# Another order of the first FFN weight loads, and another home for two addends, in a fused decoder layer

## The chip, the cores and the metric

The kernel runs on one core of a Trainium2 chip. A core has a matmul engine (TensorE, PE in the profile, with its weight loads PEld), three engines for other arithmetic (VectorE or DVE, ScalarE or ACT, GpSimd or POOL) and a queue engine (SyncE or SP) that issues DMAs. DMAs are issued from the queues of SP, POOL and, here and there, ACT; each engine and each queue takes its own instructions in order, and semaphores connect them.

The metric is the device time of one execution in microseconds, the median over several runs.

## The reference

One layer of a decoder: 512 tokens of 1024 channels, in float32. An attention branch and a pooling branch are gated, projected and added to the input, then normed. What the change touches lies in the second half, the gated MLP:

```python
a, u = jnp.split(h @ w_ffn_in[l], 2, axis=-1)          # 1024 -> 2 x 2816
a = causal_dwconv(a, conv_w[l], conv_b[l])             # width 3 along the tokens
f = (jax.nn.gelu(a, approximate=False) * u) @ w_ffn_out[l]
h = layer_norm(ALPHA * h + f, ln2_g[l], ln2_b[l])
```

## The kernel before

**Precision.** A float32 operand is cut into a rounded part `hi` (by ScalarE) and the rest `lo` (by VectorE, which needs `hi`). A product is three matmuls: hi·hi, hi·lo, lo·hi (`mm3`, line 287). Each weight tile is thus split on its way: ScalarE's `whi<-...` and then VectorE's `wlo<-...` in the profile, into one of five slots (`RING`).

**FFN, first matmul.** The 2816 channels are 22 tiles of 128. For tile f there are a weight tile `a` and a weight tile `u`; f = 0 is computed in the plain way (line 1162), and f = 1 to 21, the pairs, by a scheme with seven block products in place of eight (`seven`, line 336, and, with every step written out by hand, `Begun`, line 1333, for the pairs 1 to 3). With 1 and 2 for the halves of the 1024 input channels, the weights of a pair are

- A = [a1, a2], loaded as it is (line 213),
- X = [u1 + a1, u1 + u2], made by two DMAs: SP loads u1 twice (line 223), and then POOL issues an accumulating DMA that adds a1 and u2 from memory (line 225). The second waits until the first has landed,
- D = u2, loaded by SP (line 217),
- Y = [a1 + u1 + u2, a1 + a2 + u1 + u2], formed by VectorE in A's tile from X's second half (`form_y`, line 231; `half_sum` in the hand-written part).

A block product of 128 input channels and 256 tokens is 12 matmuls of 256 columns. The products of a pair are two with A, two with X, two with Y and one with D; they run into two PSUM banks, and between two products into the same bank ScalarE or VectorE takes out what stands there (lines 341 to 356, and 1339 to 1363). What ScalarE takes out of A's first product is an addend `y`, which VectorE adds to the bank later (lines 356 and 1360).

**Order.** From line 1122 to line 1405 VectorE, ScalarE and TensorE keep the order in which the program names their instructions (`VEC.on = ACT.on = TEN.on`); after it, and on the DMA queues throughout, a planner orders the instructions by times that it estimates. `tc.issue_after` and data dependences bind it. `more()` (line 1141) splits the next weight tile.

**Where the weights of the pairs lie.** The output of the first matmul is `fT`, 22 rows of 128x512. Pairs 1 to 4 use rows of it that are written late: `tail` (line 1213) gives them rows 19, 16, 13 and 10, two for X and the next one for D. The space of `fT` is free when the last matmul of the projection before it has run. From pair 5 on X lies in one of two tiles `xraw` and D in `draw`, in space that is free after line 1320. The loads of pairs 1 and 2 are issued by line 1227; those of pairs 3 and 4 come up as the weights before them are split (line 180). Line 1304 writes one element of pair 3's X tile by a memset in VectorE's order, so that the DMA, which overwrites it, waits for VectorE to come that far.

**Where the addends lie.** Pairs 1 to 4 keep `y` in `fT` (`first`, line 1229), pairs 5 to 21 in the two halves of a tile `p1` (128x512).

**FFN, second matmul.** Line 1417 onward: again seven products, of 11 x 6 matmuls of 512 columns each (`product`, line 1465). The first, B11, has its weights loaded into six pieces `tw` (line 1331, `load_walk`): two tiles of their own, the two `xraw`, `tw4`, which takes the space of `nT1`, and last `p1`, the sixth and half as large (in the profile `p`). From each piece, once it is split, an accumulating DMA makes the weights of the next such product. The second product's weights come through three buffers `wraw` (line 273). Another set of tiles, `t3`, is loaded during the third product (line 1451); its last piece is `t3_end`, 128x512, made at line 1327 and not used until then.

Of the kernel before, what the change touches and what calls it, by code (L numbers as in the profile page):

```python
# [17 lines left out]
D = 1024  # L18
# [5 lines left out]
NF = DFF // P  # L24
# [25 lines left out]
COVER = 2  # L50
# [23 lines left out]
def layer_kernel(ctx: ExitStack, tc: tile.TileContext, xT, x, w_v, w_c, rel_bias, invcnt, w_group,  # L74
                 pscale, w_br, w_out, lnr, w_fi, convp, w_fo, out):
    nc = tc.nc
    VEC, ACT, TEN = (InLine(tc, e) for e in (nc.vector, nc.scalar, nc.tensor))
# [27 lines left out]
    first = {"q": 0, "k": 4, "p": 8, "g": 12}  # L105
# [96 lines left out]
    coming = {q: list(pair_of) for q in "DAX"}  # L202
# [6 lines left out]
    def fetch_raw(key, q):  # L209
        a, u = pair_of[key]  # L210
        r = raws[key, q] = homes[key[0], q](key[1])
        if q == "A":
            ins = nc.sync.dma_start(r, a)
            if key == ("f", COVER // 2 + 3):
                state["A5"] = ins
        elif q == "D":
            state["D", key] = nc.sync.dma_start(r, u[:, S:])
        elif key in SUMMED:
            state["plain"] = nc.sync.dma_start(r[:, :S], u[:, :S])
        else:  # L220
            v = r.rearrange("p (a c) -> p a c", a=2)
            (pst, pn), (est, _) = u.ap
            state["plain"] = nc.sync.dma_start(
                v, bass.AP(tensor=u.tensor, offset=u.offset, ap=[[pst, pn], [0, 2], [est, S]]))
            state["acc"] = nc.gpsimd.dma_start(  # L225
                v, bass.AP(tensor=a.tensor, offset=a.offset, ap=[[pst, pn], [u.offset + S - a.offset, 2], [est, S]]),
                accum_op=ALU.add)
# [108 lines left out]
    def seven(key, whole, tt, y, u, done, between=None, begun=None, turned=False):  # L336
        ba, bc = begun or seven_a(key, whole, y)
        bb = bank(f"sb{key[0]}{key[1]}")
        chain, low, c11 = ba[:, 256:], bb[:, :256], bc[:, :256]

        def b_(k, t):
            return whole[0][:, k, t], whole[1][:, k, t]

        flush()
        s_mm(key, "X", 0, tt["T3"], low, True)
        state["low"] = nc.scalar.activation(u[:, t2], low, AF.Copy, scale=-1.0 if turned else 1.0)
        s_mm(key, "Y", 0, tt["nT2"], chain, False)
        state["Y0"] = state["mm"]
        nc.scalar.activation(u[:, t1], chain, AF.Copy)
        s_mm(key, "D", 0, tt["T4"], low, False)  # L350
        nc.vector.tensor_tensor(u[:, t1], u[:, t1], low, op=ALU.add)
        if between:
            between()
        s_mm(key, "X", 1, tt["nT1"], chain, False, between or key == ("f", NF - 1))
        nc.vector.tensor_tensor(u[:, t2], u[:, t2], chain, op=ALU.subtract if turned else ALU.add)
        state["add"] = added[key] = nc.vector.tensor_tensor(ba[:, t1], y, c11, op=ALU.add)

        def close():
            s_mm(key, "Y", 1, b_(k2, t2), chain, False, between or key == ("f", NF - 1))
            done(ba, u)  # L360

        pending.append(close)
# [558 lines left out]
    def gate_done(f, ba, u):  # L921
        if f < KT - 1:
            for br, v, scale in ((0, ba, 1.0), (1, u, -1.0)):
                nc.scalar.activation(v, v, AF.Sigmoid, scale=scale)
                nc.vector.tensor_tensor(branch[f, br], branch[f, br], v, op=ALU.mult)
            merged(f, branch[f, 0], branch[f, 1])
            unused.append(branch[f, 1])
        else:
            for br, v, scale in ((0, ba, 1.0), (1, u, -1.0)):
                gslot[8 * br + f] = unused.pop(0)  # L930
                nc.scalar.activation(gslot[8 * br + f], v, AF.Sigmoid, scale=scale)
# [6 lines left out]
    for f in range(GSEVEN, KT):  # L938
        if f == KT - 1:
# [3 lines left out]
              lambda ba, u, f=f: gate_done(f, ba, u), first_half if f == KT - 1 else None)  # L943
# [218 lines left out]
    def fi_mm(j, b, t, pin=False):  # L1162
        wh, wl = split3(weights(at["f", j // 2, "au"[j % 2]]), KT)
        for kt in range(KT):
            mm3(b[:, t], (wh[:, kt, :], wl[:, kt, :]), (hT_hi[:, kt, t], hT_lo[:, kt, t]), kt == 0, kt == KT - 1,
                pin and kt == 0)
# [18 lines left out]
    def gated(j, a, u, sign=None):  # L1185
        gate_begin(j, a)
        gate_end(j, u, sign)
# [25 lines left out]
    tail = {COVER // 2 + n: NF - 3 * (n + 1) for n in range(4)}  # L1213

    def x_home(f):
        if f in tail:
            return fT[:, tail[f]:tail[f] + 2, :].rearrange("p a c -> p (a c)")
        return xraw[f % 2]
# [2 lines left out]
        return fT[:, tail[f] + 2, :] if f in tail else draw[:, f % 2 * S:(f % 2 + 1) * S]  # L1221

    homes["f", "X"], homes["f", "D"] = x_home, d_home
    for f in list(tail)[:2]:
        for q in "XD":
            coming[q].remove(("f", f))
            fetch_raw(("f", f), q)

    def first(f):
        n = min(tail.values()) - 1 - f // 2 % 2  # L1230
        return fT[:, n, f % 2 * 256:f % 2 * 256 + 256]
# [26 lines left out]
    def low(i, *names):  # L1258
        for n in names:
            lows[n, i]()  # L1260
# [40 lines left out]
        begin_seven(2)  # L1301
    half_sum(1, 0)
    fi_mm(0, hb[0], t2)
    VEC.memset(x_home(COVER // 2 + 2)[:, :1], 0.0)
    state["mid"] = [lambda: low(2, "T4")]
    more()
    high(3, "nT2")
# [16 lines left out]
    p1 = xu.tile([P, S], F32, name="p1")  # L1324
    tw = [xu.tile([P, D], F32, name=f"tw{n}") for n in range(2)]
    tw += [xraw[(NF - 2) % 2], xraw[(NF - 1) % 2], p1]
    t3 = [xu.tile([P, S], F32, name="t3_end")]

    def load_walk(*which):
        for c in which:  # L1330
            state["walk"] = nc.sync.dma_start(tw[c], half("B11", piece(c)))
# [74 lines left out]
    pending.append(before.close)  # L1406
    state["limit"] = len(chunks) - 1
    for f in SEVEN[BEGUN:]:
        y = first(f) if f in tail else p1[:, f % 2 * 256:f % 2 * 256 + 256]
        if f == NF - 2:  # L1410
            with tc.issue_after(state["D", ("f", f - 1)].ins):
                load_walk(0, 1)
        elif f == NF - 1:
            load_walk(2)
        seven(("f", f), (hT_hi, hT_lo), tt, y, fT[:, f, :], lambda ba, u, f=f: gated(f, ba, u, -1.0),
              turned=f < KH)
# [205 lines left out]
```

## Time and profile before

| | us |
|---|---|
| median of 3 runs | 619.1 |
| the three runs | 615.93, 619.1, 621.42 |
| the profiled execution | 623.8 |
| its span, first to last instruction | 622.1 |
| TensorE busy | 608.5 |
| VectorE busy | 526.5 |
| ScalarE busy | 371.8 |
| POOL busy | 132.8 |
| mean granted TensorE clock | 0.997 of full speed |

A profile's numbers belong to one execution, which is a little longer than the three runs shown. A row of a timeline gives the start (us from the start of the span), the duration, the engine, the line, the operation and what it writes and reads; in brackets stands how long the engine was idle before and what ended that. Line 67 is a helper that records the instructions of the hand-ordered engines, so for most rows the names of the tiles tell the place: `sa..`, `sb..` are the two banks of a pair, `fi` those of tile 0, `foa` to `foe` and `fol` those of the second matmul. In the hand-ordered part each copy into `fT` is an output or an addend of a pair. A row of the chain gives start, duration and what was on it; for a DMA, from its issue to its landing. A row of a window gives the stretch, its length, the busy time of PE, PEld, DVE, ACT and POOL with their numbers of instructions, the granted clock, the busy share of the DMA engines and GB/s.

Matmuls are pipelined in the profile: a row's duration is longer than the distance to the next row's start.

### The profile page before, as it was taken

The numbers are of one execution on the slowest core, as the hardware profiler recorded it, in microseconds if no ns is written. First come the engines' busy times: TensorE is split into PE (matmuls) and PEld (weight loads), VectorE is DVE, ScalarE is ACT, GpSimd is POOL, SyncE is SP. The second block draws the span as 40 slices with busy tenths as digits, with TensorE's granted clock in tenths as the row PEclk, the third lists the DMA queues.
The fourth block names the chain that finished last, engine by engine and source line by source line (L and its number), as shares of the span: only waits on it lengthen the run. The fifth ranks groups of instructions, "written<-read, shape, count | busy, mean of one in ns | idle before, by whom it ended". The sixth has DMA issues, their size and how long they took to land.

```text
span 622.1 us, 11141 instructions
## 1 busy us (share of the span) xinstructions
PE 608.5 (98%) x4317; PEld 550.8 (89%) x4317; DVE 526.5 (85%) x808; ACT 371.8 (60%) x573; POOL 132.8 (21%) x149
## 2 busy tenths in 40 slices
PE   9999999999999999999979999999999999999995
PEld 6899898777899998889979999999999996788885
DVE  6978886868879888789969989999998985999995
ACT  6536667567556655445645666666666664755761
POOL 0133207350512111101110111102122121542110
PEclk9999999999999999999999999999999999999998
DMA  8667654147877235906692677677897687999424
GB/s 318 217 189 195 170 161 144 36 156 233 215 188 175 53 130 179 365 3 207 144 224 87 167 190 193 189 208 177 210 262 199 174 179 170 330 211 210 95 38 98
DMA packets 44228, 110.24 MB, mean 177 GB/s; under 512 B 4480, under 2 KB 6408, under 8 KB 44176
## 3 DMA queue, kind: packets, MB, share of 16 engines
q0 software_dynamic: 16576, 39.74, 32.9%
q1 hardware_dynamic: 27168, 69.15, 32.5%
q8 instruction: 34, 0.56, 0.4%
q10 hardware_dynamic: 432, 0.66, 0.3%
q14 instruction: 18, 0.15, 0.1%
HBM read 105.96 MB, written 3.69 MB: 176 GB/s over the span
## 4 chain that ended last, share of the span: by engine, by line
PE 89%; DMA 6%; DVE 2%; issue 1%; ACT 1%; SPq 0%; ACTq 0%; POOLq 0%
PE saf L67 21%; PE sbf L67 8%; PE br L67 7%; PE wo L67 7%; PE sag L67 6%; PE fod L67 5%; DMA fT<-in_w_fi 5%; PE foa L67 5%; PE sai L67 5%; PE sbg L67 3%; PE foe L67 3%; PE v L480 3%; PE sbi L67 2%; PE g L67 2%; PE p L67 2%; PE scg L67 2%
## 5 line engine op out<-in xcount | busy, mean ns | idle before, releaser
L67 ACT ACTIVATE whi<-araw 128x1024 fp32r<-128x1024 f32 x62 | 65.4, 1059 | 28.5 <-PE saf L67 14.1
L67 DVE TENSOR_TENSOR wlo<-araw,whi 128x1024 fp32r<-128x1024 f32 x62 | 75.8, 1242 | 6.2 <-ACT whi L67 4.3
L67 PE MATMUL saf<-hT_hi,whi 128*128 128x256 f32 x252 | 70.5, 280 | 0.7 <-DVE fT L67 0.7
L67 PE MATMUL saf<-hT_lo,whi 128*128 128x256 f32 x252 | 70.0, 278 | 0.0
L67 PE MATMUL saf<-hT_hi,wlo 128*128 128x256 f32 x252 | 69.8, 277 | 0.0
L225 POOL DMA_DIRECT2D xraw<-in_w_fi x17 | 20.4, 1197 | 145.7 <-DMA xraw<-in_w_fi 72.3
L67 PE MATMUL saf<-nT_hi,whi 128*128 128x256 f32 x168 | 46.7, 278 | 2.2 <-ACT fT L67 2.2
L67 DVE TENSOR_TENSOR wlo<-wraw,whi 128x1024 fp32r<-128x1024 f32 (+1 forms) x33 | 38.8, 1184 | 11.3 <-ACT whi L67 11.1
L67 PEld LDWEIGHTS saf<-hT_hi,whi 128*128 128x128 f32 x252 | 47.3, 188 | 1.0 <-DVE fT L67 0.9
L67 PEld LDWEIGHTS saf<-hT_lo,whi 128*128 128x128 f32 x252 | 47.3, 188 | 0.0
L67 PEld LDWEIGHTS saf<-hT_hi,wlo 128*128 128x128 f32 x252 | 47.3, 188 | 0.0
L67 PE MATMUL saf<-nT_lo,whi 128*128 128x256 f32 x168 | 46.8, 279 | 0.0
L67 PE MATMUL saf<-nT_hi,wlo 128*128 128x256 f32 x168 | 46.7, 278 | 0.0
L67 ACT ACTIVATE whi<-wraw 128x1024 fp32r<-128x1024 f32 (+1 forms) x33 | 33.0, 1015 | 17.9 <-DMA wraw<-in_w_out 7.5
L67 PE MATMUL sbf<-T_lo,whi 128*128 128x256 f32 x144 | 40.1, 278 | 0.0
L67 PE MATMUL sbf<-T_hi,whi 128*128 128x256 f32 x144 | 40.0, 278 | 0.0
L67 PE MATMUL sbf<-T_hi,wlo 128*128 128x256 f32 x144 | 39.9, 277 | 0.0
L67 ACT ACTIVATE whi<-xraw 128x1024 fp32r<-128x1024 f32 x25 | 26.4, 1061 | 18.6 <-PE saf L67 13.9
L67 PEld LDWEIGHTS saf<-nT_hi,whi 128*128 128x128 f32 x168 | 31.5, 188 | 2.4 <-ACT fT L67 2.4
L67 DVE TENSOR_TENSOR wlo<-xraw,whi 128x1024 fp32r<-128x1024 f32 x25 | 30.7, 1233 | 1.3 <-ACT whi L67 0.2
L67 PEld LDWEIGHTS saf<-nT_hi,wlo 128*128 128x128 f32 x168 | 31.5, 188 | 0.0
L67 PEld LDWEIGHTS saf<-nT_lo,whi 128*128 128x128 f32 x168 | 31.5, 188 | 0.0
(455 smaller groups left out, 2111.1 us busy)
## 6 DMA issues: line engine op xcount, KB each, us to landing
araw<-in_w_fi SPq DMA_DIRECT2D x19, 512.0 KB, 4.1
xraw<-in_w_fi SPq DMA_DIRECT2D x17, 512.0 KB, 5.9
xraw<-in_w_fi POOLq DMA_DIRECT2D x17, 512.0 KB, 7.1
araw<-in_w_c SPq DMA_DIRECT2D x12, 512.0 KB, 5.2
tw<-in_w_fo POOLq DMA_DIRECT2D x9, 512.0 KB, 9.3
draw<-in_w_fi SPq DMA_DIRECT2D x17, 256.0 KB, 3.6
wraw<-in_w_br SPq DMA_DIRECT2D x8, 512.0 KB, 4.2
wraw<-in_w_out SPq DMA_DIRECT2D x8, 512.0 KB, 4.0
```

Source lines behind the costliest of these rows:

```text
L67: ins = call(*a, **kw)
L225: state["acc"] = nc.gpsimd.dma_start(v, bass.AP(tensor=a.tensor, offset=a.offset, ap=[[pst, pn], [u.offset + S - a.offset, 2], [est, S]]), ...
L480: ins = nc.tensor.matmul(bs[j], xs_[j][a], (wh, wl)[b], start=kt == 0 and n == 0, stop=False)
```

## The change

Three edits.

1. The loop that issues the loads of pairs 1 and 2 (X1 with its accumulation, D1, X2, D2) now issues those of pairs 1 to 3 in the order X1, X2, D1, X3, D2, D3.
2. The memset of line 1304 writes into pair 4's X tile instead of pair 3's, so that pair 4's load waits for it.
3. The addends of the pairs 20 and 21 lie in `t3[0]`, which at that place is `t3_end`, instead of `p1`.

```diff
     homes["f", "X"], homes["f", "D"] = x_home, d_home
-    for f in list(tail)[:2]:
-        for q in "XD":
-            coming[q].remove(("f", f))
-            fetch_raw(("f", f), q)
+    for q, n in (("X", 0), ("X", 1), ("D", 0), ("X", 2), ("D", 1), ("D", 2)):
+        key = ("f", COVER // 2 + n)
+        coming[q].remove(key)
+        fetch_raw(key, q)
...
-    VEC.memset(x_home(COVER // 2 + 2)[:, :1], 0.0)
+    VEC.memset(x_home(COVER // 2 + 3)[:, :1], 0.0)
...
     for f in SEVEN[BEGUN:]:
-        y = first(f) if f in tail else p1[:, f % 2 * 256:f % 2 * 256 + 256]
+        home = p1 if f < NF - 2 else t3[0]
+        y = first(f) if f in tail else home[:, f % 2 * 256:f % 2 * 256 + 256]
```

`COVER // 2` is 1 and `NF` is 22, so `COVER // 2 + 2` is pair 3 and `NF - 2` is pair 20.

## The prediction

> **What bounds the kernel now.** I read four views: the page for the share of each engine, the timeline of TensorE (PE) for its idle stretches, the chain of waits around them, and the timelines of the engines and of the two DMA queues there. "X3" is short for the X weights of pair 3, and so on.
>
> ```profile
> span 622.1 us, 11141 instructions
> PE 608.5 (98%) x4317; PEld 550.8 (89%) x4317; DVE 526.5 (85%) x808; ACT 371.8 (60%) x573; POOL 132.8 (21%) x149
> ```
>
> TensorE is the bound, so the change can win only where TensorE stands still. After the first 6 us and before the last 6 it does so six times, in two places:
>
> ```profile
> 319.23 0.39 PE L67 MATMUL saf<-nT_hi,whi 128*128 128x256 f32 x1 [2.25 <-ACT fT L67]
> 321.90 0.38 PE L67 MATMUL sb<-T_hi,wlo 128*128 128x256 f32 x1 [0.77 <-DVE wlo L67]
> 324.03 0.39 PE L67 MATMUL saf<-hT_hi,whi 128*128 128x256 f32 x1 [0.69 <-DVE fT L67]
> ...
> 520.30 0.73 PE L67 MATMUL foa<-whi,T_hi 128*128 128x512 f32 x2 [0.71 <-ACT whi L67]
> 523.65 0.50 PE L67 MATMUL fob<-wlo,hT_hi 128*128 128x512 f32 x1 [0.72 <-DVE wlo L67]
> 535.47 0.73 PE L67 MATMUL fod<-whi,T_hi 128*128 128x512 f32 x2 [0.65 <-ACT whi L67]
> ```
>
> The brackets add up to 5.8 us, but the slow matmuls beside them (0.73 where others take 0.28 or 0.39) hide more, so I take the loss from the steady pace. A matmul of 256 columns starts every 3.93/34 = 0.1156 us, one of 512 columns every 14.96/66 = 0.2267 us:
>
> ```profile
> 348.11 3.93 PE saf L67 x34
> ...
> 504.58 8.40 PE foa L67 x37
> ...
> 569.31 14.96 PE fod L67 x66
> ...
> 599.23 2.72 PE fol L67 x12
> ```
> ```profile
> 305.73:328.77 23.04, 19.33 (x163) 18.73 (x161) 18.07 (x27) 12.33 (x20) 3.56 (x3) 1.00 0.69 162
> ```
>
> The window runs from the first matmul of pair 1's X to pair 3's second X product; its 163 records are 160 matmuls and three at the edges. 160 x 0.1156 = 18.5 us of work in 23.04: place one loses **4.5 us**. From the start of the output products (504.58) to the last of them (599.23) there are 6 products of 66 matmuls and 12 small ones: 396 x 0.2267 + 12 x 0.1156 = 91.2 us in 94.65: place two loses **3.5 us**. The granted clock is 1.00 in the window, so it is not the throttle.
>
> Place one, the cause, on the chain, ScalarE (ACT), VectorE (DVE) and the SP queue:
>
> ```profile
> 285.65 0.38 SPq L223 DMA_DIRECT2D fT<-in_w_fi  x1
> ...
> 288.30 0.54 SPq L223 DMA_DIRECT2D fT<-in_w_fi  x1
> ```
> ```profile
> 302.38 5.14 DMA fT<-in_w_fi
> ...
> 308.44 9.39 DMA fT<-in_w_fi
> ```
> ```profile
> 302.29 0.06 DVE L67 MEMSET fT<- 128x1 f32 x1
> ...
> 317.85 0.69 DVE L67 TENSOR_TENSOR araw<-fT,araw 128x512 f32<-128x512 f32 x1 [4.87 <-DMA fT<-in_w_fi]
> ...
> 323.56 0.41 DVE L67 TENSOR_TENSOR fT<-fT,saf 128x256 f32<-128x256 f32 x1
> ```
> ```profile
> 313.14 0.78 ACT L67 ACTIVATE y<-fi,cvp 128x512 f32<-128x512 f32 x1
> 317.85 1.06 ACT L67 ACTIVATE whi<-fT 128x1024 fp32r<-128x1024 f32 x1 [3.93 <-DMA fT<-in_w_fi]
> 318.81 0.37 ACT L67 ACTIVATE fT<-saf 128x256 f32<-128x256 f32 x1
> ...
> 325.62 1.06 ACT L67 ACTIVATE whi<-fT 128x1024 fp32r<-128x1024 f32 x1 [0.24 <-PE saf L67]
> ```
>
> X1, X2 and X4 go out in one burst from 285.65 (X4 at 288.30). X3 stands behind the one-element memset of line 1304: loaded at 302.38, its accumulating half issued at 308.44, landed at 317.83. ACT's split of X3 (317.85) and DVE's half sum of pair 3 (317.85) wait for it in program order; behind ACT's split stands the copy of pair 2's accumulator (318.81), for which TensorE waits.
>
> **The change, part by part.** *X3 into the burst, X4 behind the memset.* Nothing is added: the same twelve DMAs (of each pair the load of X, the load of D and the accumulation), in another order on SP, and the memset on another tile. SP sees X1, X2, D1, X3, D2, D3 and then D4; the burst holds as many bytes as before, since X3 takes X4's place. POOL still issues four accumulations in turn, X3's now third:
>
> ```profile
> 296.47 1.18 POOL L225 DMA_DIRECT2D fT<-in_w_fi  x1 [2.70 <-DMA fT<-in_w_fi]
> 308.44 1.19 POOL L225 DMA_DIRECT2D fT<-in_w_fi  x1 [10.78 <-DVE wlo L67]
> 314.89 1.18 POOL L225 DMA_DIRECT2D xraw<-in_w_fi  x1 [5.27 <-DMA xraw<-in_w_fi]
> ```
>
> X4's was issued at 296.47; X3's comes no later, and with the longest landing seen here (9.39) it is there by 306. Its readers come free at 312.98 (DVE: 317.85 - 4.87) and 313.92 (ACT: 317.85 - 3.93), so 7 us cover it. Then DVE runs its unbroken row of work 4.87 earlier: pair 2's subtraction, now at 323.56, would be ready to run at 318.7. TensorE without the wait starts pair 2's second X product at 316.8 (12 matmuls after the last D product, 319.23 - 2.25 - 0.16), ends it at 318.2, does X of pair 3 until 319.6 and then needs that subtraction, which ends at 319.1. Place one closes with half a microsecond of spare; I take all 4.5, bounds 3.5 (a spare so thin fails and a wait of 0.7 like that at 324.03 stays, with its restart) and 4.5.
>
> What pays for it: X1 and X2 share the burst with X3 and D1 waits behind X2. Pair 1 is the tight one:
>
> ```profile
> 301.65 0.69 DVE L67 TENSOR_TENSOR own<-fT,own 128x512 f32<-128x512 f32 x1 [0.53 <-DMA fT<-in_w_fi]
> ...
> 302.87 1.22 DVE L67 TENSOR_TENSOR wlo<-fT,whi 128x1024 fp32r<-128x1024 f32 x1
> ```
>
> DVE waits 0.53 for X2 and splits X1 until 304.09, TensorE needs it at 305.73: 1.6 us of cover. X2 leaves SP one place earlier than before, which helps, and X3 two places before X4 did, which hurts. I cost the two together at nothing, and at 0.4 if X1 landed 2 us later, beyond its cover. X4 gets X3's old times: landed at 317.8. ACT takes it at 325.62, 4.5 earlier in the new kernel: 321.1. It is late next, with 3.3 us of cover.
>
> By the Trainium skill (DMA: Bandwidth & Descriptors, Anatomy of one DMA — SWDGE path) a DMA costs about 2.0 us and its bytes at 436 GB/s, an estimate of 3.2 us for 512 KB. By that X3 would have landed at 311.6 and place one would have no wait, so the first term would be 0 and the sum 3.5. The trace has 9.39 us and the wait, so the trace decides.
>
> *The addends of pairs 20 and 21 in t3_end instead of p1.* They are written by ACT and added by DVE at the same size, cost 0. What goes is a reader of p1, which is also the last slice (128x512) of the output weights' first product:
>
> ```profile
> 504.61 0.33 SPq L1331 DMA_DIRECT2D tw<-in_w_fo  x1
> 510.58 0.33 SPq L1331 DMA_DIRECT2D p<-in_w_fo  x1
> 523.62 3.91 SPq L273 DMA_DIRECT2D wraw<-in_w_fo  x3
> ```
> ```profile
> 487.71 0.43 DVE L356 TENSOR_TENSOR saf<-p,saf 128x256 f32<-128x256 f32 x1
> 496.98 0.43 DVE L356 TENSOR_TENSOR saf<-p,saf 128x256 f32<-128x256 f32 x1
> 510.09 0.43 DVE L356 TENSOR_TENSOR saf<-p,saf 128x256 f32<-128x256 f32 x1
> ```
> ```profile
> p<-in_w_fo SPq DMA_DIRECT2D x1, 256.0 KB, 9.0
> ```
> ```profile
> 511.17 1.06 ACT L67 ACTIVATE whi<-tw 128x1024 fp32r<-128x1024 f32 x1 [3.79 <-DMA tw<-in_w_fo]
> 519.62 0.63 ACT L67 ACTIVATE whi<-p 128x512 fp32r<-128x512 f32 x1 [7.39 <-PE foa L67]
> ```
>
> The load left at 510.58, right after pair 21's sum (510.09 + 0.43); 9.0 us later, at 519.6, ACT split it, and TensorE needed it at 519.6. The row names PE, but the landing falls on the same moment. With the new home only pair 19's sum (487.71) holds it. If the planner leaves it behind tw on SP it goes at 504.9 and lands by 513.9; if it moves it forward, before 500. Either way ACT can split it after tw, at 512.1 or 513.9, 5.7 us or more before TensorE's need. ACT, idle since 512.2, goes on at once with the second product's weights, which now wait behind p, so the three wraw loads of 523.62 leave about as much earlier and the waits at 523.65 and 535.47 go too. t3_end's own load comes after those and after 510.5: no wait. All **3.5** go; bounds 0 (the PE named in the row was the real releaser) and 3.5. I see nothing that is late there next.
>
> Sum: 4.5 + 3.5 = 8.0. The profiled execution took 623.8 us (span 622.1 and 1.7 around it): 615.8.
>
> That execution is 4.7 above the median (619.1) and 2.4 above the slowest of the three runs. Either the median run has the same waits, and comes to 611.1; or TensorE's own work is the same in each and the spread of 5.5 us is the waits, so the fastest run (615.93) had hardly any and the median ends at 615.8. Nothing in one trace tells these apart; I take the middle, **613.5**, 5.6 under the median, that is 0.7 of the profile's 8.0, and use that 0.7 below.
>
> **The rivals.** (1) The p1 part does nothing, as ACT's split at 519.62 waits for TensorE to free a slot of the five in its ring. For: the row says so. Against: the landing at 519.6 explains it, and TensorE had long read the earlier slices of this product out of their slots. Then 4.5 x 0.7 = 3.2 off: 615.9.
> (2) X4 becomes what X3 was. Its accumulation shares the queue with pairs 5 and 6 (314.89), and beyond 321.1 it stops ACT in program order. For: same time, same traffic, 9.39 to land. Against: 3.3 us of cover. It gives back up to 4.5: 3.5 x 0.7 = 2.5 off: 616.6.
> (3) The waits are there under the profiler and hardly without: hidden, nothing changes, 619.
> (4) The other side: the planner lays out pairs 4 to 21 anew (from line 1405 nothing is pinned) and puts a late DVE step in front of TensorE in each pair. For: DVE is nearly full there. Against: no TensorE wait between 328.77 and 519.6 under the present order, and the change gives the loop nothing new to order.
>
> ```profile
> 348.10:357.82 9.72, 9.72 (x87) 9.72 (x86) 9.34 (x14) 5.78 (x10) 1.20 (x1) 1.00 0.68 207
> ```
>
> 9.34 of 9.72 us are DVE's, 0.38 spare. To end 1% over the median (625.3) it must cost 11.8 over 18 pairs, 0.66 in each, which is more than the spare; from 0.31 a pair on it eats the gain.
>
> A rule that speaks against the first part is the Trainium skill's (DMA: Bandwidth & Descriptors, Issuing engines are not separate DMA queues): DMAs of SP and POOL run on the same 16 engines and interleave, so an earlier X3 slows X1 and X2. By it X1 comes late only if the burst grew; X3 takes X4's place, so the volume agrees with before, and the sum stays.
>
> **How the numbers follow.** A measurement here can tell about 1%: faster means under 612.9, slower over 625.3. Both waits go: 0.72, between 611.1 and 615.8 with some scatter to each side; a little under half of that lies below 612.9, so 0.34 is faster and 0.38 the same. Rival 1: 0.08, rival 2: 0.06, rival 3: 0.08, all within 1%. Rival 4: 0.06, slower. Together 0.34, 0.60, 0.06. The range 610.0 to 617.5 holds the first case but 0.06 at its ends, and rivals 1 and 2; left out are 3 and 4: 0.20.
>
> **What would show it.** Right: X3's accumulation issued by 297 and no TensorE wait between 305 and 330, the window's 23.04 us at about 18.5; the load of p issued at 505 or earlier, ACT's split of p by 514, no TensorE wait between 504 and 540, and 504.58 to 599.23 shrunk to about 91.2. Wrong: a wait of ACT for fT at pair 4 (rival 2); ACT's split of p still at the end of the matmuls before it though p landed long ago (rival 1); waits that return in each of pairs 4 to 21 (rival 4); a trace without waits but a time that stays (rival 3).

## The result, and the profile after

| | before | after |
|---|---|---|
| median (us), 17 runs of each side by side | 621.34 | 616.21 |
| range of these runs | 615.93 to 623.78 | 615.62 to 617.41 |
| the profiled execution | 623.8 | 615.82 |
| its span | 622.1 | 614.1 |

The ratio of the times is 0.9936 with a 95% interval from 0.9916 to 0.9956: 0.6% faster. The means of the 17 runs give the same ratio (620.3 and 616.3, 4.0 us); the medians lie 5.1 us apart, since before's runs are spread wider and unevenly. The prediction's 613.5 is 2.7 too low, its range (610.0 to 617.5) holds the time. The best run has hardly moved (615.93 to 615.62); the long runs are gone. The profiled execution came to 615.82 where the sum made against before's, the slowest of its 17 runs, said 615.8.

First the page of the kernel after, then what its view of waits lists for TensorE (in all, times, longest):

```profile
span 614.1 us, 11143 instructions
...
PE 606.5 (99%) x4317; PEld 551.0 (90%) x4317; DVE 527.0 (86%) x808; ACT 371.8 (61%) x573; POOL 132.8 (22%) x149
```
```profile
PE by_pe L1054 <- ACT draw L1053: 1.9, 1, 1.9
PE warm_ps L394 <- PEq L1615: 0.8, 1, 0.8
```

Of the six waits of before in the two places none is left: one at the start and one in the last 6 us are all. Both stretches now run at the steady pace. The view of windows (us; busy time of each engine; granted clock; DMA share) for place one and place two:

```profile
305.48:323.97 18.49, 18.49 (x163) 18.49 (x161) 17.95 (x27) 12.14 (x20) 3.56 (x3) 1.00 0.74 175
499.61:590.79 91.18, 91.18 (x411) 75.73 (x409) 84.10 (x92) 60.90 (x73) 25.34 (x27) 1.00 0.84 189
```

23.04 became 18.49 and 94.65 became 91.18: 4.55 + 3.47 = 8.0 us. The rows behind it, on POOL, ScalarE, VectorE and SP:

```profile
293.62 1.18 POOL L225 DMA_DIRECT2D fT<-in_w_fi  x1 [1.09 <-DMA fT<-in_w_fi]
307.52 1.19 POOL L225 DMA_DIRECT2D fT<-in_w_fi  x1 [12.71 <-DVE T_lo L67]
```
```profile
313.55 1.06 ACT L67 ACTIVATE whi<-fT 128x1024 fp32r<-128x1024 f32 x1
...
321.44 1.06 ACT L67 ACTIVATE whi<-fT 128x1024 fp32r<-128x1024 f32 x1
```
```profile
312.72 0.69 DVE L67 TENSOR_TENSOR araw<-fT,araw 128x512 f32<-128x512 f32 x1
...
318.64 0.41 DVE L67 TENSOR_TENSOR fT<-fT,saf 128x256 f32<-128x256 f32 x1
```
```profile
482.93 0.33 SPq L1331 DMA_DIRECT2D p<-in_w_fo  x1
...
499.81 0.33 SPq L1331 DMA_DIRECT2D tw<-in_w_fo  x1
```
```profile
505.78 1.06 ACT L67 ACTIVATE whi<-tw 128x1024 fp32r<-128x1024 f32 x1 [3.21 <-DMA tw<-in_w_fo]
506.75 0.62 ACT L67 ACTIVATE whi<-p 128x512 fp32r<-128x512 f32 x1
```

X3's accumulation now leaves at 293.62 (308.44 before), X4's at 307.52. ScalarE's splits of X3 (313.55) and of X4 (321.44) and VectorE's half sum of pair 3 (312.72) stand without a bracket: the profile shows no wait. The planner has put p's load 17 us ahead of the last `tw`, and ScalarE splits p right behind `tw`.

### The profile page after: what moved, and what is told of

It is laid out like the page before. It is cut to its first block, busy times and chain, and to the rows that moved or that the text cites. A ratio compares the mean times of both kernels' runs of the same rounds, so it can differ in the third digit from the quotient of the medians.

```text
span 614.1 us, 11143 instructions
## 1 busy us (share of the span) xinstructions
PE 606.5 (99%) x4317; PEld 551.0 (90%) x4317; DVE 527.0 (86%) x808; ACT 371.8 (61%) x573; POOL 132.8 (22%) x149
## 4 chain that ended last, share of the span: by engine, by line
PE 98%; DVE 1%; DMA 1%; issue 0%
PE saf L67 24%; PE sbf L67 8%; PE br L67 7%; PE wo L67 7%; PE sag L67 6%; PE foa L67 5%; PE fod L67 5%; PE sai L67 5%; PE sbg L67 3%; PE foe L67 3%; PE v L480 3%; PE fob L67 2%; PE sbi L67 2%; PE fi L67 2%; PE g L67 2%; PE p L67 2%
## 5 line engine op out<-in xcount | busy, mean ns | idle before, releaser
L67 DVE TENSOR_TENSOR wlo<-wraw,whi 128x1024 fp32r<-128x1024 f32 (+1 forms) x33 | 38.7, 1183 | 12.8 <-ACT whi L67 12.6
L67 DVE SCALAR_TENSOR_TENSOR y<-saf,cvp,y 128x511 f32<-128x511 f32 (+1 forms) x42 | 31.2, 744 | 0.3 <-ACT y L67 0.3
```

Source lines behind the costliest of these rows:

```text
L67: ins = call(*a, **kw)
```

## The experiments

Twelve kernels ran, in three sets of four, each set beside the kernel before on one chip. That kernel alone varied: medians of 617.31 (35 runs), 619.21 (34) and 617.84 (32) beside the 621.34 above, single runs from 615.47 to 626.74. So what follows is read from ranges and windows as much as from medians, and times of different sets are compared with care. The theory: TensorE's own work, about 615.5 us, is a floor; place one and place two are separate waits on separate loads; a run pays for whichever load lands late in it. The rivals: the wait at place two comes from TensorE's slots, not from p's load; X4 is as tight as X3 was; the scatter has nothing to do with the two places.

**The parts alone.** Edits 1 and 2 (the loads), and edit 3 (the addends' home), each once in the first and once in the third set.

`e1_loads` and `e11_loads_2`: the kernel after with

```diff
-        home = p1 if f < NF - 2 else t3[0]
-        y = first(f) if f in tail else home[:, f % 2 * 256:f % 2 * 256 + 256]
+        y = first(f) if f in tail else p1[:, f % 2 * 256:f % 2 * 256 + 256]
```

> The first two edits alone (order of the loads of pairs 1 to 3, memset on pair 4); the addends of pairs 20 and 21 stay in p1. Theory (two independent waits, each worth what TensorE lost in it): no TensorE wait between 305 and 330, the loss of about 3.5 us between the first output product and the last stays, the time falls by about the first wait's share of the 4 to 5 us that the whole change is worth, 2 to 3 us, and the runs still scatter, since the second wait is left. Rival (only the home of the addends counts in unprofiled runs): the time stays within 1 us of before and the runs scatter as before.

> Edits 1 and 2 alone (the loads), on the chip of e10 and e12. Theory: place one is gone and place two stays, so no run is over 619 (of the kernel before a third of the runs are over 620), and the median lies 0.5 to 1.5 us over the changed kernel's 616.2 to 616.6. Rival (both places make the slow runs): some of 12 runs at 620 or over.

`e2_home` and `e12_home_2`: the kernel before with

```diff
-        y = first(f) if f in tail else p1[:, f % 2 * 256:f % 2 * 256 + 256]
+        home = p1 if f < NF - 2 else t3[0]
+        y = first(f) if f in tail else home[:, f % 2 * 256:f % 2 * 256 + 256]
```

> The third edit alone (addends of pairs 20 and 21 in t3_end); loads and memset as before. Theory: the load of p is issued before 500, no TensorE wait in the output products (6 products in about 91.2 us instead of 94.7), the waits of 0.7 to 2.3 us at pair 2 and 3 stay; the time falls by 1.5 to 3 us. Rival (ACT's split of p waited for a slot that TensorE frees): the split of p stays at the end of the matmuls before it, and the time stays. The two parts together should add up to the whole change within 1 us.

> Edit 3 alone (the addends' new home). Theory: place one stays, so the runs lie on both sides, some at 615.6 to 617, the others at 620 to 622, as many as X3 is late in; the best runs are as fast as the changed kernel's. Rival: all runs within 2 us of each other, which would put the slow runs in place two.

| kernel | median | range, 12 runs each | ratio to before, 95% interval |
|---|---|---|---|
| e1_loads | 617.56 | 615.94 to 618.40 | 0.9986, 0.9956 to 1.0016 |
| e11_loads_2 | 617.80 | 616.18 to 618.49 | 0.9978, 0.9953 to 1.0003 |
| e2_home | 616.26 | 615.61 to 621.41 | 0.9988, 0.9954 to 1.0023 |
| e12_home_2 | 616.59 | 615.54 to 620.91 | 0.9967, 0.9939 to 0.9995 |

By the ratio three of the four can't be told from before, and `e12_home_2` only just; the falls of the median that were expected in the first set, 2 to 3 us and 1.5 to 3, did not come (0.3 up and 1.1 down), as only 10 of before's 35 runs there are at 620 or over. The ranges tell the kernels apart. With the loads alone no run of 24 is over 618.5. With the new home alone the 24 runs fall into two groups with nothing between: 16 from 615.54 to 616.82, and 8 from 619.53 to 621.41. One group is at the floor, the other 4 to 5 us above it. The profiled execution of `e2_home` is one of the first group, that of `e12_home_2` one of the second. Place one of `e2_home`, then of `e12_home_2`, by windows:

```profile
305.40:323.89 18.49, 18.49 (x162) 18.49 (x161) 17.63 (x27) 11.71 (x19) 3.56 (x3) 1.00 0.79 187
```
```profile
305.72:328.68 22.96, 20.61 (x162) 20.21 (x161) 17.87 (x27) 12.03 (x19) 3.56 (x3) 0.93 0.67 161
```

22.96 - 18.49 = 4.5 us is place one by itself, in one and the same kernel; the spans differ by as much (618.5 and 613.9). And 622.1 of before less 618.5 is 3.6: place two, which this kernel doesn't have. Its output products, by windows, are at the pace of the kernel after:

```profile
504.33:595.50 91.17, 91.17 (x410) 75.72 (x409) 84.08 (x92) 61.03 (x73) 25.37 (x27) 1.00 0.84 189
```

So both terms of the sum were measured: 4.5 in one kernel with and without it, 3.5 as the difference between two kernels.

What differs between the two executions, on POOL, SP and VectorE, first `e2_home`:

```profile
306.60 1.19 POOL L225 DMA_DIRECT2D fT<-in_w_fi  x1 [9.51 <-DVE nT_lo L67]
```
```profile
308.22 0.38 SPq L223 DMA_DIRECT2D xraw<-in_w_fi  x1
```
```profile
312.68 0.69 DVE L67 TENSOR_TENSOR araw<-fT,araw 128x512 f32<-128x512 f32 x1 [0.36 <-DMA fT<-in_w_fi]
```

and `e12_home_2`:

```profile
308.53 1.19 POOL L225 DMA_DIRECT2D fT<-in_w_fi  x1 [10.94 <-DVE wlo L67]
```
```profile
308.72 0.38 SPq L223 DMA_DIRECT2D xraw<-in_w_fi  x1
...
310.13 0.47 SPq L217 DMA_DIRECT2D draw<-in_w_fi  x1
```
```profile
317.77 0.69 DVE L67 TENSOR_TENSOR araw<-fT,araw 128x512 f32<-128x512 f32 x1 [4.98 <-DMA fT<-in_w_fi]
```

X3's accumulation leaves 1.9 us later and ends 5.1 later: 6.1 us from issue to its reader when it goes 1.6 ahead of SP's loads for pairs 5 and 6, 9.2 when it goes beside them (9.4 in the kernel before, issued at 308.44). A slip of 2 us grows to 5. The other traces, where X4 is the held one, bear it out. In each of the ten executions below SP's next load leaves 6.5 us after the held load; what differs is how far the accumulation goes ahead of it:

| accumulation ahead of SP's next load (us) | issue to landing (us) | executions |
|---|---|---|
| 1.2 to 1.8 | 5.8 to 6.2 | e2_home, after, e3_home_held, e6_pair_order, e9_p_later |
| 1.0 | 7.2 | e11_loads_2 |
| 0.2 to 0.6 | 9.1 to 9.4 | before, e12_home_2, e1_loads, e7_after |

(In `e10_x3_twice`, below, it left 1.9 us behind that load and took 8.6.) Such a jump fits the two groups with nothing between; that every long run had it is not shown, since only profiled executions have a trace. By the Trainium skill (DMA: Bandwidth & Descriptors, Issuing engines are not separate DMA queues) transfers of POOL and SP interleave on the same engines; these rows agree, with 3.1 us for company. The held load itself lands 4.0 us after its issue in `e2_home` and 5.4 in `e12_home_2`. Why, stays open; this difference of 1.4 us starts the slip.

**Place one enlarged.** `e10_x3_twice`, `e2_home` with the held load of X3 issued twice, one behind the other:

```diff
-            state["plain"] = nc.sync.dma_start(
-                v, bass.AP(tensor=u.tensor, offset=u.offset, ap=[[pst, pn], [0, 2], [est, S]]))
+            for _ in range(2 if key == ("f", COVER // 2 + 2) else 1):
+                state["plain"] = nc.sync.dma_start(v, bass.AP(tensor=u.tensor, offset=u.offset, ap=[[pst, pn], [0, 2], [est, S]]))
```

> The kernel before with edit 3 (the addends' new home), and the held load of X3 issued twice, one behind the other (512 KB more, the same bytes), so that its accumulation leaves about 4 us later, at 310.6. Place one alone, with the cause doubled and everything kept that is computed. Theory (beyond 312.7 TensorE loses what X3 lands later, one for one): with landings of 6.1 to 9.4 us X3 is there at 316.7 to 320, so 3.5 to 7.5 us are lost in every run: median 619.5 to 622.5, none under 618.5. Rival (X3's landing does not set the slow runs): under 618.

Median 622.96, 12 runs from 621.3 to 624.62, ratio 1.0066 (1.0044 to 1.0089): no run is left at the floor, and the median is 0.5 over what was expected at most. Its rows on POOL and VectorE, and place one by windows:

```profile
311.04 1.19 POOL L225 DMA_DIRECT2D fT<-in_w_fi  x1 [13.03 <-DVE wlo L67]
```
```profile
319.67 0.69 DVE L67 TENSOR_TENSOR araw<-fT,araw 128x512 f32<-128x512 f32 x1 [6.42 <-DMA fT<-in_w_fi]
```
```profile
306.32:331.39 25.07, 21.60 (x163) 21.40 (x161) 17.94 (x28) 11.86 (x19) 3.56 (x3) 0.86 0.68 168
```

VectorE waits 0.36, 4.98 and 6.42 us in the three executions, and place one loses 0, 4.5 and 6.6. X3's landing sets place one. From the second to the third, 1.44 of wait cost 2.1: TensorE has no other wait in the window, and the rest goes with the lower clock (0.86; last section).

`e8_x3_later` was to hold X3 longer by moving its memset down:

```diff
-    VEC.memset(x_home(COVER // 2 + 2)[:, :1], 0.0)
     state["mid"] = [lambda: low(2, "T4")]
...
     state["mid"] = [lambda: low(3, "nT2")]
     more()
+    VEC.memset(x_home(COVER // 2 + 2)[:, :1], 0.0)
```

> The kernel before with edit 3 (the addends' new home) and with X3's memset 4.0 us later in VectorE's order (301.6 to about 305.6). Place one alone, with the cause doubled. Theory (TensorE loses what X3 lands after 312.5, one for one, in every run): with landings of 6.1 to 9.4 us X3 lands at 316.7 to 320, 4 to 7.5 us are lost in each run, none is below 619, median 620 to 622. Rival (X3's landing is not what sets the slow runs of the kernel before): the time moves by less than 2 us, median under 618.5, and runs of 615.6 remain.

It did something else. In the new place the memset, which writes one column (128x1), stands behind the program's own load of X3, so it held nothing: all four X went in one burst, the fourth from SP at 289.16, and the memset, at 307.93, set the first column of pair 3's X to zero before it was read. Median 617.99 (617.48 to 619.28). So it says nothing on X3's landing and is a second case of the next experiment.

**No X held back.** `e4_all_burst`, the kernel after without the memset:

```diff
-    VEC.memset(x_home(COVER // 2 + 3)[:, :1], 0.0)
```

> The changed kernel without any memset: the loads of all four pairs X1 to X4 go out in the first burst. Theory (the burst is limited by the DMA engines, so one X more delays the others): X1's or X2's accumulation lands up to 2 us later than 299 and 301.5, beyond the 1.6 us of cover TensorE waits at pair 1, and the time rises by 0 to 2 us. Rival (there is room in the burst): the time stays within 0.5 us of the changed kernel, and holding pair 4 back is worth nothing.

Median 617.49, 12 runs from 616.96 to 617.92. VectorE's waits for X1 and X2, TensorE's wait and place one by windows:

```profile
300.64 0.69 DVE L67 TENSOR_TENSOR own<-fT,own 128x512 f32<-128x512 f32 x1 [1.05 <-DMA fT<-in_w_fi]
303.72 0.69 DVE L67 TENSOR_TENSOR own<-fT,own 128x512 f32<-128x512 f32 x1 [1.06 <-DMA fT<-in_w_fi]
```
```profile
308.54 0.39 PE L67 MATMUL saf<-nT_hi,wlo 128*128 128x256 f32 x1 [0.52 <-DVE wlo L67]
```
```profile
306.24:326.16 19.92, 19.25 (x163) 18.72 (x161) 19.41 (x29) 12.94 (x21) 2.37 (x2) 1.00 0.67 168
```

A fourth X in the burst makes VectorE wait 2.1 us for X1 and X2 (0.53 before) and costs 19.92 - 18.49 = 1.4 us, in the order of after; in the order of before (`e8_x3_later`) the same window is 19.91. The hold itself is worth 1.4 us, whichever order the loads have.

**The order, and X4's cover.** `e6_pair_order`, the kernel after with

```diff
-    for q, n in (("X", 0), ("X", 1), ("D", 0), ("X", 2), ("D", 1), ("D", 2)):
+    for q, n in (("X", 0), ("D", 0), ("X", 1), ("D", 1), ("X", 2), ("D", 2)):
```

> The changed kernel with the burst in the order of the pairs (X, D of pair 1, X, D of pair 2, X, D of pair 3) and still pair 4's X held. It tests the reason given for costing X1 and X2 at nothing, that X2 leaves one place earlier. Theory: the landing follows the number of bytes ahead in the burst, so X2 lands some 0.4 us later and X3 0.4 to 1 later, both inside their cover: 616 to 617, no wait of TensorE. Rival (the order does the work, not the hold): a TensorE wait at pair 1 or 2 near 308 as in e4_all_burst, and 617 to 618.5.

Median 615.66, 9 runs from 615.41 to 616.31, ratio 0.9943 (0.9919 to 0.9968); place one takes 18.50 us, and VectorE waits 0.52 us for X2 as in the kernel after: X2 isn't later, where 0.4 us had been expected. So edit 1's order does none of the work; that X3 is in the burst and X4 is not does all of it. The runs lie lower and closer than those of after in two other sets (616.21 and 616.57), but not beside them, and its one profile has a span of 613.8 against 614.1, a difference that is there before place one begins. Whether it is the better order stays open.

`e5_x4_late`, the kernel after with X4's memset 7 us later:

```diff
     low(3, "nT1")
     half_sum(1, 1)
+    VEC.memset(x_home(COVER // 2 + 3)[:, :1], 0.0)
     more()
```

> The changed kernel with the memset that holds pair 4's X some 7 us later in VectorE's order (302.1 to about 309.2). This tests the third step's cover of X4, which ended at 321.1 to 321.4. Theory: X4's load leaves at about 309.3, its accumulation at 314 and lands between 320 and 323.5, so ScalarE's split of pair 4 waits 0 to 2 us for it and the time grows by as much, 616 to 618; one row in the profile of ScalarE waiting for the DMA of fT near 321. Rival (this end of the queue has no scatter that matters, X4 always lands in 6.2 us): 615.7 to 616.5 and no such row.

Median 616.44 (615.85 to 617.35), beside 616.57 of the kernel after. On SP, POOL and ScalarE:

```profile
309.36 0.38 SPq L223 DMA_DIRECT2D fT<-in_w_fi  x1
```
```profile
315.64 1.19 POOL L225 DMA_DIRECT2D fT<-in_w_fi  x1 [20.45 <-DVE y L67]
```
```profile
320.66 1.06 ACT L67 ACTIVATE whi<-araw 128x1024 fp32r<-128x1024 f32 x1
321.76 1.06 ACT L67 ACTIVATE whi<-fT 128x1024 fp32r<-128x1024 f32 x1
```

X4's accumulation left 8.1 us later than in the kernel after, behind all of SP's loads, and took 6.0 us: it landed at 321.6, as the theory had it. ScalarE's split of X4 starts 1.10 us after the split before it, where 0.94 to 0.96 is the pace in seven other traces, so it waited some 0.15 us, and the time shows nothing of it. That is the end of X4's cover. The rival's reason, a landing always in 6.2 us, falls: in `e7_after` and `e1_loads` X4 took 9.1 and 9.4 us, landed at 317.3 and 318.0, and ScalarE took it at 321.42 and 321.95 without a wait.

`e7_after`, the kernel after again:

> The changed kernel again, beside three variations and the kernel before on one chip. Theory (TensorE's own work, about 615.6 us, is a floor, and each single execution adds to it what the late loads cost it that time): median 615.7 to 617, no run over 618, while runs of the kernel before reach 620 to 623. Rival (the spread is in the machine and not in the two waits): the changed kernel has runs of 620 and over here too.

Median 616.57, 11 runs from 615.63 to 617.01, ratio 0.9947 (0.9925 to 0.997), beside runs of before up to 626.74.

**Place two.** `e3_home_held`, the kernel after with p1 held behind pair 21's sum as before, though no addend lies in it:

```diff
+    with tc.issue_after(added["f", NF - 1].ins):
+        nc.vector.memset(p1[:, :1], 0.0)
     load_walk(3, 4, 5)
```

> The changed kernel, with one more memset of one element of p1 on VectorE behind pair 21's sum, so that the load of p leaves where it left before although the addends no longer lie in p1. Theory (it is the time of this load, not the home of the addends): the loss of about 3.5 us in the output products comes back in the profile, the time is 1.5 to 3 us over the changed kernel's, and so within 1 us of the first two edits alone. Rival (the tile itself or the planner's other order does it): the time stays at the changed kernel's 616.

`e9_p_later`, the same, and p loaded twice, one load behind the other:

```diff
-    load_walk(3, 4, 5)
+    load_walk(3, 4, 5, 5)
```

> The changed kernel with p held behind pair 21's sum as in e3_home_held and then loaded twice, one load after the other (the same bytes, 256 KB more). Place two alone, with its cause doubled: the second load leaves at about 512.8 and lands at about 519.5, 5 us after TensorE needs the slice (514.7). Theory (the load of p and what stands behind it on SP set the second wait): a wait of TensorE of 4 to 8 us between 512 and 535, median 620 to 624, no run under 619. Rival (the wait at the end of the first output product came from TensorE's own slots, as the row of the kernel before names PE): under 617.5.

Medians 617.03 (615.62 to 618.95) and 622.08 (620.41 to 624.19; ratio 1.0036, 1.0006 to 1.0066). For four executions follow p's issue to landing in the list of DMA issues (the last number; not for `e9_p_later`, which loads it twice), ScalarE's split of p, and the output products by windows.

`e3_home_held`:

```profile
p<-in_w_fo SPq DMA_DIRECT2D x1, 256.0 KB, 6.5
```
```profile
512.85 0.63 ACT L67 ACTIVATE whi<-p 128x512 fp32r<-128x512 f32 x1 [5.89 <-PE foa L67]
```
```profile
500.05:591.40 91.35, 91.35 (x410) 75.67 (x409) 83.95 (x93) 60.87 (x73) 25.30 (x27) 1.00 0.84 191
```

`e1_loads`:

```profile
p<-in_w_fo SPq DMA_DIRECT2D x1, 256.0 KB, 7.1
```
```profile
513.47 0.63 ACT L67 ACTIVATE whi<-p 128x512 fp32r<-128x512 f32 x1 [5.59 <-DMA p<-in_w_fo]
```
```profile
500.12:591.97 91.85, 91.47 (x410) 75.67 (x409) 83.87 (x92) 60.80 (x73) 25.35 (x27) 1.00 0.84 190
```

`e11_loads_2`:

```profile
p<-in_w_fo SPq DMA_DIRECT2D x1, 256.0 KB, 8.1
```
```profile
513.99 0.63 ACT L67 ACTIVATE whi<-p 128x512 fp32r<-128x512 f32 x1 [7.40 <-DMA p<-in_w_fo]
```
```profile
499.60:592.50 92.90, 92.19 (x410) 75.41 (x409) 83.80 (x92) 60.80 (x73) 24.81 (x27) 1.00 0.83 188
```

`e9_p_later`:

```profile
516.72 0.63 ACT L67 ACTIVATE whi<-p 128x512 fp32r<-128x512 f32 x1 [1.87 <-DMA p<-in_w_fo]
```
```profile
499.88:595.21 95.33, 93.00 (x411) 76.59 (x409) 85.24 (x93) 59.64 (x73) 24.67 (x27) 0.98 0.82 187
```

Counted from the start of the output products, against 91.18 us in the kernel after:

| execution | split of p after (us) | place two loses (us) |
|---|---|---|
| after | 7.1 | 0 |
| e3_home_held | 12.8 | 0.2 |
| e1_loads | 13.4 | 0.7 |
| e11_loads_2 | 14.4 | 1.7 |
| before | 15.0 | 3.5 |
| e9_p_later | 16.8 | 4.2 |

The expectation of `e3_home_held` missed: the load of p left where it did before, 6.2 us after the start of the output products (6.0 in before, 6.2 in the two kernels of the loads alone), but only 0.2 us was lost, not 3.5, and the median lies 0.5 to 0.8 over those of the kernel after (of other sets), not 1.5 to 3. Nor did 3.5 us stay in `e1_loads` (0.7). What differs is how long p took to land: 9.0 us in before, 8.1, 7.1 and 6.5 here, against 3.1 in the kernel after, where it leaves 17 us ahead of the output products. So a late issue makes the loss possible, and the landing in the single execution sets its size. Why it takes 6.5 to 9.0 us stays open.

In `e9_p_later` the second load took only some 4 us, so p came earlier than expected and TensorE's wait is 2.33 us, not 4 to 8; the loss of 4.2 and the median are those expected, as the clock fell behind the wait (last section).

The loss rises with p's split, from about 13 us on. Where the row names PE (in before, and here in `e3_home_held`), the kernel after refutes it: there the same split ran 7.1 us after the start and waited for nothing. p had landed only 0.1 us or less before the split in both (510.58 + 9.0, and 506.24 + 6.5): the releaser named was the event that happened to fall last, not the cause.

## Why the prediction was right, and where it was off

*What bounds the kernel.* Right: the two places lost 4.5 and 3.5 us in that execution, and each was found again (`e12_home_2`; before less `e12_home_2`). One reading beside it is off: the rows of 0.73 us are two matmuls in one row (x2; at full pace such a row takes 0.62), so they were not slow by as much as the text says. The loss was taken from the steady pace, so no term hangs on it.

*X3 into the burst.* Right. Its accumulation leaves by 297 (293.62), place one closes (18.49 against 18.5 forecast), pair 2's subtraction starts at 318.64 (318.7 forecast), and the bound of 3.5 for a spare that fails was not needed.

*X1 and X2 at nothing.* Right in size: VectorE waits 0.52 us for X2 where it waited 0.53. The reason given, bytes in the burst, held, since one X more costs 1.4 us; the worry over places on SP was idle, as `e6_pair_order` shows.

*X4 late next, with 3.3 us of cover.* About right where X4 lands slowly: 318.0 and 317.3 in `e1_loads` and `e7_after` (317.8 forecast), 3.9 and 4.1 us before its split. Where it lands in 6.2 us, as in the profile of the kernel after, the cover is 7.7. `e5_x4_late`, with a landing of 6.0 us, used all of it up.

*The addends' home.* Right: all 3.5 us of the profiled execution, and the planner moved the load forward. In other executions place two is smaller: 0.7 and 1.7 in the two profiles of the loads alone, whose medians stand 1.0 to 1.6 above the kernel after's.

*The rivals.* (1), the slot in the ring, falls by the table of place two. (2), X4, falls: it landed as late as the rival had it in two traces and nothing waited. (3), waits that hardly exist without the profiler, falls too, since the time fell, but has a grain of truth: an execution need not have them. (4): the planner moved p's load, and no wait came up in pairs 4 to 21.

*From the profile to the median.* This is the step that failed: "I take the middle, 613.5, 5.6 under the median, that is 0.7 of the profile's 8.0". There was no middle. Of the two readings the text named, the second held: the sum, 615.8, is close to a floor. No run of any kernel here is under 615.4, and the waits are what a run of before has on top of it. Of 118 runs of before 43 are at 620 or over (9 of 17 in the set of the result, 10 of 35, 12 of 34, 12 of 32). By the groups of edit 3 alone, those should be the runs with place one; that is inferred, as only profiled executions show their waits. So the median of before moves with that share, between 617 and 621, and so does the gain; the median of after doesn't. That the sum and the fastest of three runs (615.93) agreed to 0.1 us was the evidence for the floor, and it was given half weight; 0.34 for "faster by over 1%" rested on the reading that fell. The range holds 616.21 with some luck: it lies above the 615.8 at which the forecast's own case ended, in the part kept for scatter and for two rivals that did not come. What spreads the runs of after over 615.6 to 617.4 stays open.

## What to carry to other kernels

A kernel whose runs scatter by 1% while TensorE is 98% busy may have a floor and a wait that comes and goes: take the waits out of the one profiled execution, and if what is left equals the fastest run, forecast that, not a share of the gain. A load that is issued just beside a burst of others is a good one to move: here a slip of 2 us in its start became 5 us in its end, and which transfers flew together counted, not their order within the burst. A releaser named in a row is only the last event by time, so ask whether the same instruction ever ran early without it.

## What the runs showed of the hardware beyond that

A stop of TensorE can cost more than its length. Place one of `e12_home_2`, TensorE's rows and the windows of the stop, of the 3.3 us behind it and of the next 1.5:

```profile
319.15 0.52 PE L67 MATMUL saf<-nT_hi,whi 128*128 128x256 f32 x1 [2.18 <-ACT fT L67]
319.47 0.41 PE L67 MATMUL saf<-nT_lo,whi 128*128 128x256 f32 x1
319.68 0.41 PE L67 MATMUL saf<-nT_hi,wlo 128*128 128x256 f32 x1
```
```profile
317.00:319.15 2.15, 0.00 (x0) 0.00 (x1) 1.35 (x3) 1.33 (x2) 0.37 (x1) 1.00 1.11 300
319.15:322.46 3.31, 3.31 (x16) 3.31 (x17) 3.27 (x7) 2.14 (x3) 0.82 (x1) 0.51 0.96 153
322.46:324.00 1.54, 1.36 (x11) 1.16 (x10) 1.54 (x3) 0.19 (x1) 0.00 (x0) 0.94 0.99 181
```

After a stop of 2.18 us the granted clock was 0.51 for 3.3 us, and matmuls started every 0.21 us instead of 0.1156. The window behind the stop of 2.33 us in `e9_p_later`, the one behind the stop of 2.25 us in the kernel before, at the place of `e12_home_2`'s, and the one behind the longer stop of 3.47 us in `e10_x3_twice`:

```profile
517.40:520.13 2.73, 2.73 (x7) 2.11 (x7) 2.48 (x3) 2.73 (x4) 0.86 (x1) 0.50 0.13 9
```
```profile
319.23:320.91 1.68, 1.68 (x14) 1.68 (x14) 1.65 (x4) 1.61 (x3) 1.19 (x1) 1.00 1.02 187
```
```profile
321.05:327.19 6.14, 6.14 (x29) 6.14 (x29) 5.97 (x11) 2.75 (x5) 0.00 (x0) 0.50 0.59 118
```

They show 0.50, 1.00 and 0.50, the last for 6.1 us. So the clock fell after some stops of 2.2 to 2.3 us and not after others. By the Trainium skill (TensorE: Matmul & The Clock Gate, HAM oscillation — how this bites in real kernels) the stops to avoid are those of more than about 3.4 us; the stop of 3.47 us agrees, but 2.2 to 2.3 us were enough in two of three executions, and the measurement decides. In `e12_home_2` the half clock cost little, since TensorE had VectorE's late subtraction to wait for anyway: it loses 4.5 us with the half clock, as the kernel before does without it.
